# A two-layer encoder trunk: in layer 1 the weights of the strips and gate pairs are split one step sooner, the latent norms run piece by piece, and value tiles and the second key strip stand in front of the rope strip

## The chip, the cores and the metric

The kernel runs on one core of a Trainium2 chip. A core has a matrix engine (TensorE, "PE" in the profile), a vector engine ("DVE"), a scalar engine ("ACT"), a general engine ("POOL") and a queue that issues most DMAs ("SP"). Each engine works through its own list of instructions strictly in order and waits on semaphores for the others. The metric is the device time of one execution in microseconds; lower is better. The kernel before takes 1453.56 us (median of 3 runs, 1452.67 to 1453.84).

## What is computed

A sequence of 1024 tokens of width 1024 goes through two layers and a final RMSNorm. Both layers have an adaLN modulation, a SiLU gate z and a gated residual add. Layer 0 mixes tokens by differential attention, layer 1 by multi-head latent attention. Only layer 1 is touched by the change:

```python
proj = h @ w_in                      # q_a (384) | c_kv (256) | k_pe (64) | z (1024)
q  = (_rmsnorm(q_a, q_a_norm_g) @ w_q_b).reshape(b, s, 8, 128 + 64)
q_nope = q[..., :128]; q_pe = _rope(q[..., 128:], positions)
k_pe = _rope(k_pe[:, :, None, :], positions)[:, :, 0]
kv = (_rmsnorm(c_kv, kv_a_norm_g) @ w_kv_b).reshape(b, s, 8, 128 + 128)
k_nope, v = kv[..., :128], kv[..., 128:]
sc = (q_nope @ k_nope^T + q_pe @ k_pe^T) * scale      # per head
o  = softmax(sc) @ v
y  = (o.reshape(b, s, 1024) * silu(z)) @ w_out
x  = x + gate * y                    # then the final RMSNorm
```

## The kernel before

**Number format.** Every operand of a product is held as a pair of fp32r tiles, "hi" (the rounded value, suffix `h`) and "lo" (what is left, suffix `l`). One product is three matmuls (`mm3`: hi by hi, hi by lo, lo by hi; L180 to L182). A tile is 128 partitions by 512 values. Activations are kept transposed (features on partitions, tokens in two halves of 512).

**Weights.** A weight strip is 128 columns of the input projection. It comes in two pieces of 256 KB (`fetch_strip`, tile `wraw`, two buffers). `split_raw` makes the pair of a piece: ACT casts the hi tile (`wh`, L225), POOL subtracts for the lo tile (`wl`, L226). The pairs live in a ring of six tiles (tag `whl`). `gen_half` then runs one half of the tokens against one strip in eight steps of three matmuls; `side.tick()` after each step lets pending small work out of a queue (`side`).

**Layer 1, in order.** Layer 1 takes its strips in this order: k_pe (which goes through rope), the gates z of heads 0 and 1 (strips 6 and 7), and the two strips of c_kv (4 and 5). Beside these, `combos()` prepares sums of the activations (`t1` to `t4`, on DVE and ACT). Then come three gate pairs (`z_pair`), each two heads by seven products of 12 matmuls in the manner of Strassen; their weights (`zraw`, then the sums of them at L1372 to L1375) come from `z_weights`. Next are the three strips of q_a, with value tiles between them, then the key, rope and query strips of the heads (`kn`, `qr`, `qn`), and the attention loop, which uses later strips as filler between its steps (`stream1`).

**Latent norms.** `lora` normalises c_kv (2 tiles of features, `craw` to the pair `ck`) and q_a (3 tiles, `cqr` to `cq`), for each half of the tokens. The chain of one half is: sums of squares, `cps` (four tiny matmuls, L1302), `c_w` on DVE (L1304), `rq_y` on POOL (L167), a DMA `bc_d` to memory (L403), a DMA `bc_s` that broadcasts it back to all partitions (L405), one multiplication of each feature tile on DVE (L1311), and the split on ACT and DVE (L1319, L1320). The pieces of this chain stand in a list `norms`, and `run_norms()` issues what is in it at chosen places.

**Value tiles.** `v1_tile(tt, fh)` is six matmuls into `vps`; ACT and DVE make `v_hl` from it (L357, L358) and a DMA stores it. There are 8 token tiles for each of two halves `fh` of the value columns; I call those of fh 0 t0 to t7 and those of fh 1 f0 to f7. `load_wk` loads their weights (`wvr`, in the same two buffers as the strips) and splits them: `wvh` on DVE (L1436) and `wvl` on POOL (L1437).

**What sets the order.** The order in which the program is written decides most, then a scheduler places each engine's instructions from it. Accumulators (`acc`, `zacc`, `vps`) rotate through five PSUM banks here, so a product waits until the one five back has been read out by ACT and DVE.

## Time and profile before

| | |
|---|---|
| time, median of 3 runs | 1453.56 us (1452.67 to 1453.84) |
| profiled execution, its own time | 1448.94 us |
| span inside that execution | 1447.2 us |
| PE busy | 1392.7 us, 96% |
| PE weight loads | 1161.4 us, 80% |
| DVE busy | 913.5 us, 63% |
| ACT busy | 733.6 us, 51% |
| POOL busy | 609.6 us, 42% |

The profiled execution is 1.74 us longer than its span and 4.62 us (0.32%) shorter than the median. Times below are microseconds from the start of the span. A row of a timeline gives the start, the duration, the engine, the line, the operation, output and input tiles and, in square brackets, how long the engine stood idle before it and which instruction released it. Matmuls are pipelined: a row's duration is longer than the step from one start to the next, and where a length of matmuls is meant, the text goes by starts.

### The profile page before, as it was taken

The page shows a single profiled execution, that of the slowest core. Times are in us where ns is not written, and L with a number is a line of the kernel's source. Part 1 is how long each engine was busy: PE and PEld are TensorE (multiplying, and loading weights), DVE is VectorE, ACT ScalarE, POOL GpSimd, SP SyncE. Part 2 cuts the span into 40 slices and gives each one's busy share as a digit, 9 for nine tenths or more (in the row PEclk, how much of TensorE's full clock was granted, in tenths as well). Part 3 has the DMA queues.
Part 4 walks back from the last instruction along what each step waited for, and adds up shares of the span by engine and source line. Part 5 has one row for each costly group of instructions (what it writes and reads, how often), then busy time and mean ns, then how long its engine had stood idle before and what let it go on. Part 6 is the DMA issues. An engine that isn't in the chain of part 4 may idle for free.

```text
span 1447.2 us, 20558 instructions
## 1 busy us (share of the span) xinstructions
PE 1392.7 (96%) x7388; PEld 1161.4 (80%) x7388; DVE 913.5 (63%) x1360; ACT 733.6 (51%) x1299; POOL 609.6 (42%) x483
## 2 busy tenths in 40 slices
PE   5999999999999999998999998988999999999997
PEld 4777788888888887887787776867888888888886
DVE  6657877767777767677355965254666555555355
ACT  5622375656566655566344533334454554545442
POOL 4415164656465555553651246312141321412562
PEclk9999999999999999999999999999999999999999
DMA  9788823333332424237753322565343432336663
GB/s 330 231 258 231 254 72 96 81 98 91 100 92 83 110 74 116 57 91 263 235 164 131 88 73 88 163 175 138 119 127 114 122 101 76 104 96 215 216 206 138
DMA packets 129766, 203.20 MB, mean 140 GB/s; under 512 B 18432, under 2 KB 55424, under 8 KB 129664
## 3 DMA queue, kind: packets, MB, share of 16 engines
q1 hardware_dynamic: 129664, 201.89, 46.1%
q8 instruction: 58, 0.95, 0.3%
q14 instruction: 44, 0.36, 0.1%
HBM read 132.68 MB, written 45.56 MB: 123 GB/s over the span
## 4 chain that ended last, share of the span: by engine, by line
PE 78%; DMA 7%; DVE 6%; issue 3%; ACT 2%; POOL 2%; SPq 1%; ACTq 0%; POOLq 0%; DVEq 0%
PE s L1567 10%; PE acc L182 8%; PE acc L181 8%; PE acc L180 8%; PE tr L378 7%; PE s L769 7%; PE pv L180 4%; PE pv L181 4%; PE pv L182 4%; PE oacc L181 3%; PE oacc L180 3%; PE oacc L182 3%; DMA wvr<-in_w_v 1%; PE zacc L182 1%; DMA ada<-in_ada_ss 1%
## 5 line engine op out<-in xcount | busy, mean ns | idle before, releaser
L380 ACT CAST pth<-tr 128x512 fp32r<-128x512 f32 x256 | 150.1, 587 | 283.9 <-PE tr L378 279.4
L395 DVE TENSOR_REDUCE nm<-s 128x1 f32<-128x1024 f32 x192 | 233.8, 1218 | 74.0 <-PE s L769 64.1
L381 DVE TENSOR_TENSOR ptl<-tr,pth 128x512 fp32r<-128x512 f32 x256 | 175.9, 687 | 139.3 <-ACT pth L380 138.6
L226 POOL TENSOR_TENSOR wl<-wraw,wh 128x512 fp32r<-128x512 f32 (+2 forms) x82 | 104.0, 1270 | 216.3 <-ACT wh L225 197.2
L378 PE MATMUL tr<-ident,e 128*128 128x128 f32 x1024 | 155.1, 274 | 5.8 <-ACT e L397 3.8
L378 PEld LDWEIGHTS tr<-ident,e 128*128 128x128 f32 x1024 | 121.5, 141 | 46.4 <-DVE ptl L381 18.6
L397 ACT ACTIVATE e<-s,nm 128x1024 f32<-128x1024 f32 x128 | 143.5, 1121 | 28.6 <-DVE nm L395 28.2
L180 PE MATMUL acc<-h0h,wh 128*128 128x512 f32 x360 | 150.0, 417 | 3.6 <-DVE v_hl L358 2.6
L180 PE MATMUL pv<-pth,vt 128*128 128x256 f32 x512 | 147.2, 288 | 0.0
L181 PE MATMUL pv<-ptl,vt 128*128 128x256 f32 x512 | 145.8, 285 | 0.0
L182 PE MATMUL pv<-pth,vt 128*128 128x256 f32 x512 | 144.7, 283 | 0.0
L182 PE MATMUL acc<-h0h,wl 128*128 128x512 f32 x360 | 142.2, 395 | 0.2 <-POOL wl L226 0.2
L181 PE MATMUL acc<-h0l,wh 128*128 128x512 f32 x360 | 141.4, 393 | 0.0
L1009 POOL TENSOR_TENSOR wol<-wor,woh 128x512 fp32r<-128x512 f32 x64 | 85.2, 1350 | 84.4 <-ACT woh L1008 79.1
L180 PEld LDWEIGHTS pv<-pth,vt 128*128 128x128 f32 x512 | 97.6, 191 | 3.1 <-ACT pth L380 0.4
L181 PEld LDWEIGHTS pv<-ptl,vt 128*128 128x128 f32 x512 | 97.7, 191 | 2.6
L182 PEld LDWEIGHTS pv<-pth,vt 128*128 128x128 f32 x512 | 97.7, 191 | 0.1
L322 POOL TENSOR_TENSOR rp_r<-rp_raw,cosT 128x512 f32<-128x512 f32 x38 | 49.8, 1310 | 98.4 <-ACT rp_raw L317 51.9
L327 POOL TENSOR_TENSOR rp_sw<-rp_sw,sinT 128x512 f32<-128x512 f32 x42 | 56.0, 1333 | 78.0 <-DMA rp_sw<-rp_raw 73.3
L769 PE MATMUL s<-ks,qa 128*128 128x512 f32 x256 | 82.0, 402 | 3.0 <-DVE e L777 2.6
L777 DVE SCALAR_TENSOR_TENSOR e<-s,z,e 128x1024 f32<-128x1024 f32 x64 | 82.1, 1283 | 2.1
L769 PE MATMUL s<-ks,qb 128*128 128x512 f32 x256 | 80.9, 394 | 0.0
(600 smaller groups left out, 3344.2 us busy)
## 6 DMA issues: line engine op xcount, KB each, us to landing
ada<-in_ada_ss SPq DMA_DIRECT2D x32, 512.0 KB, 6.0
wraw<-in_w_s SPq DMA_DIRECT2D x64, 256.0 KB, 3.0
vS<-v_hl SPq DMA_DIRECT2D x32, 512.0 KB, 5.0
vt<-vS SPq DMA_DIRECT2D x32, 512.0 KB, 3.8
wor<-in_w_out SPq DMA_DIRECT2D x64, 256.0 KB, 4.1
rp_sw<-rp_raw SPq DMA_DIRECT2D x168, 64.0 KB, 2.0
bc_s<-bc_d SPq DMA_DIRECT2D x34, 256.0 KB, 4.2
oS<-bc_s SPq DMA_DIRECT2D x30, 256.0 KB, 2.9
```

The costliest lines, as they stand in the source:

```text
L180: PE.matmul(psum, ah, bh, start=first, stop=False)
L181: PE.matmul(psum, ah, bl, start=False, stop=False)
L182: PE.matmul(psum, al, bh, start=False, stop=last)
L226: sub = (V if pair_of else G).tensor_sub(l_[:, :n], raw[:, :n], f32v(h_[:, :n]))
L378: PE.transpose(tr[:, j, :], p[:, kt * P : (kt + 1) * P], ident)
L380: mk["S"] = S.copy(pth[kh][:, :, dst], tr).ins
L381: mk["V"] = V.tensor_sub(ptl[kh][:, :, dst], tr, f32v(pth[kh][:, :, dst])).ins
L395: mk["V"] = V.reduce_max(nm, s_ps, axis=AX.X, negate=True).ins
L397: mk["S"] = S.activation(e, s_ps, AF.Exp, bias=nm, scale=1.0, accum_out=zs).ins
L769: PE.matmul(s_ps[:, kc * HF : (kc + 1) * HF], src[:, c, ql], KS[h][kc][:, c, :], start=fst, stop=not fst)
L1009: in_turn(G.tensor_sub(lo, raw, f32v(hi)))
L1567: PE.matmul(s_ps[:, kc * HF : (kc + 1) * HF], lhs, rhs(kc), start=i == 0, stop=i == 4)
```

## The change

The computation, the instructions and their counts are the same; their order in layer 1 is not.

- `half_and_norm` becomes `run_half`, which takes hooks at given steps; `ahead()` fetches the next strip's two pieces and splits them at steps 0 and 5 of the half before it. The combos go out at every second tick, not every fourth, and `G_LATE` puts one more empty tick ahead of a group of h chunks.
- `lora`: for c_kv, scaling and split go out one feature tile at a time. For q_a the three scalings still go together.
- `z_weights` issues three of the four sums of a gate pair's weights at once, in front of its first split; `z_fetch(p + 1)` fetches all four pieces together. `load_wk(1)` moves from behind gate pair 1 to the end of pair 3, next to `load_wk(0)`.
- The second key strip goes ahead of the first rope strip and the first query strip. The q_a steps are dealt out 8 after each of the first four value tiles of fh 0 (4 after each of eight before), so the last four of them, which stood ahead of the norm of q_a, now stand beside and behind it.

```diff
@@ -45,7 +45,8 @@
 V_LATE = 6
 MODS = (2, 2, 2, 2, 3, 2, 0, 0)
 QA_V = 16
-V1_AT = ((2, 4), (3, 6), (0, 6), (1, 0))
+V_IN = 4
+V1_AT = ((2, 4), (3, 4), (0, 6), (0, 6))
 OT1_AT = 5
 NORM_AT = 4
 PRE0 = (0, 0, 0, 0, 0, 0, 1, 1, 1, 2, 1)
@@ -58,7 +59,7 @@
 Z_LAST = 4
 FILL7 = ((0, 1, 1, 1, 1, 0),) * 4
 G_WAIT = 3
-G_LATE = 2
+G_LATE = 3
 G1_AT = 7
 VB = (2, 5)
 WV1 = 6
@@ -1267,12 +1268,24 @@
             norms.remove(f)
             f()
 
-    def half_and_norm(w, half, consume):
+    def run_half(w, half, consume, at={}):
 
         for k, _ in enumerate(gen_half(w, h1, half, consume)):
             side.tick()
             if k == NORM_AT:
                 run_norms()
+            if k in at:
+                at[k]()
+
+    def ahead(raws):
+
+        hi, lo = [], []
+
+        def part():
+            for a, b in zip((hi, lo), split_raw(*raws.pop(0))):
+                a += b
+
+        return (hi, lo), {0: part, 5: part}
 
     def lora(n, dst, gvec, width, raw, part, lag):
 
@@ -1305,19 +1318,22 @@
             y = rsqrt(wv, 4)
             _, rb = bcast_rows(wp, y, "rp", 6)
 
-            def scale():
-                for i in range(n):
-                    t = craw[i][half]
-                    tc.keep_in_program_order(V.scalar_tensor_tensor(
-                        out=t3(t), in0=t3(t), scalar=gvec[:, i : i + 1], in1=rb, op0=ALU.mult, op1=ALU.mult))
-                norms.append(split)
-
-            def split():
-                for i in range(n):
-                    t = craw[i][half]
-                    dst[i][half] = hi, lo = part(), part()
-                    S.copy(hi, t)
-                    V.tensor_sub(lo, t, f32v(hi))
+            def scale(i=0):
+                t = craw[i][half]
+                tc.keep_in_program_order(V.scalar_tensor_tensor(
+                    out=t3(t), in0=t3(t), scalar=gvec[:, i : i + 1], in1=rb, op0=ALU.mult, op1=ALU.mult))
+                if i + 1 < n:
+                    if n == 2:
+                        norms.append(lambda: scale(i + 1))
+                    else:
+                        scale(i + 1)
+                norms.append(lambda: split(i))
+
+            def split(i):
+                t = craw[i][half]
+                dst[i][half] = hi, lo = part(), part()
+                S.copy(hi, t)
+                V.tensor_sub(lo, t, f32v(hi))
 
             norms.append(scale)
 
@@ -1338,40 +1354,36 @@
     cg = combos()
     side.add(None, g0)
     for i in range(16):
-        side.add(None, None, lambda: next(cg), None)
-    half_and_norm(w4[0], 1, lambda acc: side.q.insert(8, kp_half(1, acc)))
-    half_and_norm(w4[1], 1, z_put(0, 1))
-    w = strip1(7)
-    for half in range(2):
-        half_and_norm(w, half, z_put(1, half))
+        side.add(None, lambda: next(cg), None)
+    raws = fetch_strip([A["w_s1"][7, f] for f in range(2)], [4, 4])
+    run_half(w4[0], 1, lambda acc: side.q.insert(8, kp_half(1, acc)))
+    w, at = ahead(raws)
+    run_half(w4[1], 1, z_put(0, 1), at)
+    run_half(w, 0, z_put(1, 0))
+    raws = fetch_strip([A["w_s1"][4, f] for f in range(2)], [4, 4])
+    w_, at = ahead(raws)
+    run_half(w, 1, z_put(1, 1), at)
+    w = w_
     zraw = []
 
-    def z_fetch(p, parts):
-        for m, f in parts:
+    def z_fetch(p):
+        for m, f in ((0, 0), (0, 1), (1, 0), (1, 1)):
             raw = p4.tile([P, HF], F32, name="zraw", tag="zraw", bufs=6)
             SP.dma_start(raw, A["w_s1"][6 + 2 * p + m, f])
             zraw.append(raw)
 
-    for i in range(2):
-        w = strip1(4 + i)
-        for half in range(2):
-            half_and_norm(w, half, lambda acc: ckput(i, half, acc))
-            if i and not half:
-                z_fetch(1, ((0, 0), (0, 1), (1, 0), (1, 1)))
-    side.flush()
-
     def z_weights():
 
         for _ in range(1, NH // 2):
-            a11, a12 = zraw[:2]
-            yield split_raw(a11, 4)
-            yield split_raw(a12, 4)
-            a21, a22 = zraw[2:4]
+            a11, a12, a21, a22 = zraw[:4]
             del zraw[:4]
+            w_ = split_raw(a11, 4)
             s1 = p4.tile([P, HF], F32, name="zs1", tag="zraw", bufs=6)
             V.tensor_add(s1, a21, a22)
             V.tensor_sub(a21, a11, a21)
             V.tensor_sub(a11, s1, a11)
+            yield w_
+            yield split_raw(a12, 4)
             V.tensor_sub(a12, a12, a11)
             for t in (a11, a21, s1, a22, a12):
                 yield split_raw(t, 4)
@@ -1387,7 +1399,15 @@
 
     qraw = []
     zw = z_weights()
-    zq = [next(zw), next(zw)]
+    zq = []
+    run_half(w, 0, lambda acc: ckput(0, 0, acc))
+    w_, at = ahead(fetch_strip([A["w_s1"][5, f] for f in range(2)], [4, 4]))
+    run_half(w, 1, lambda acc: ckput(0, 1, acc), at)
+    side.flush()
+    z_fetch(1)
+    run_half(w_, 0, lambda acc: ckput(1, 0, acc))
+    run_half(w_, 1, lambda acc: ckput(1, 1, acc), {k: lambda: zq.append(next(zw)) for k in (0, 5)})
+
     def product(rhs):
 
         hi, lo = zq.pop(0)
@@ -1408,7 +1428,7 @@
         V.tensor_add(u, product(TC[2]), u)
         late(0)
         if more:
-            z_fetch(p + 1, ((0, 0), (0, 1)))
+            z_fetch(p + 1)
         acc = product(TC[3])
         u3 = rpt("zu3")
         V.tensor_add(u3, acc, u)
@@ -1419,8 +1439,6 @@
         V.tensor_add(u, acc, u)
         gate_out(2 * p + 1, 1, c_, c_)
         late(2)
-        if more:
-            z_fetch(p + 1, ((1, 0), (1, 1)))
         V.tensor_add(u3, product(TC[4]), u3)
         gate_out(2 * p + 1, 0, u3, u3)
         V.tensor_add(u, product(h1q(1, 1)), u)
@@ -1454,9 +1472,9 @@
             qraw.extend(fetch_strip([A["w_s1"][1, f] for f in range(2)], [4, 4]))
         if i == 2:
             load_wk(0)
+            load_wk(1)
 
     z_pair(1, late_z)
-    load_wk(1)
     z_pair(2, late_z)
     z_pair(3, late_q)
     st4.close()
@@ -1546,6 +1564,9 @@
         if h % 2 == 0:
             items.insert(len(items) - 1, (strip_l1("w_qr", h // 2, 3), CQ, qp_done(h)))
         steps1.append(16 if h % 2 == 0 else 10)
+    items[4:7] = [items[6], items[4], items[5]]
+    steps1[0] += 4
+    steps1[1] -= 4
     stream1 = Stream(gen_strips(items, wqa))
 
     def scores1(h, half, ti, zz):
@@ -1617,13 +1638,12 @@
     stream1.step(QA_V)
     for tt in range(NT):
         v1_tile(tt, 0, p4)
-        stream1.step(4)
-        if tt % 2:
-            run_norms()
+        run_norms()
+        if tt < V_IN:
+            stream1.step(32 // V_IN)
     st4.close()
     sth.close()
     ap = pool(st5, "attn1")
-    stream1.step(0)
     v1_left = list(range(NT))
     for n, steps in V1_AT:
         for tt in v1_left[:n]:
```

Three places show how the instructions now stand. Line numbers after the change are higher than before (L1311 becomes L1323, L1374 becomes L1384).

The first is DVE between gate pairs 1 and 2. `craw` is the scaling of c_kv's tiles, `zu` and `z` (L1385 before, L1397 after) belong to the gates, and the last row in each makes the weight tile that pair 2's third product needs. Before:

```order
L1311 SCALAR_TENSOR_TENSOR craw<-craw,vec,bc_s 128x512 x2
L1419 TENSOR_TENSOR zu<-zacc,zu 128x512
L1385 SCALAR_TENSOR_TENSOR z_8522<-zth,z_8522 128x512
L1320 TENSOR_TENSOR ck<-craw,ck 128x512
L1424 TENSOR_TENSOR zu_8488<-zacc,zu_8488 128x512
L1320 TENSOR_TENSOR ck<-craw,ck 128x512
L1311 SCALAR_TENSOR_TENSOR craw<-craw,vec,bc_s 128x512 x2
L1385 SCALAR_TENSOR_TENSOR zu_8488<-zth,zu_8488 128x512
L1426 TENSOR_TENSOR zu<-zacc,zu 128x512
L1436 CAST wvh<-wvr 128x512
L1374 TENSOR_TENSOR zraw<-zs_8600,zraw 128x512
```

After the change:

```order
L1323 SCALAR_TENSOR_TENSOR craw<-craw,vec,bc_s 128x512
L1439 TENSOR_TENSOR zu<-zacc,zu 128x512
L1397 SCALAR_TENSOR_TENSOR z_8525<-zth,z_8525 128x512
L1323 SCALAR_TENSOR_TENSOR craw<-craw,vec,bc_s 128x512
L1336 TENSOR_TENSOR ck<-craw,ck 128x512
L1323 SCALAR_TENSOR_TENSOR craw<-craw,vec,bc_s 128x512
L1384 TENSOR_TENSOR zraw<-zs_8542,zraw 128x512
```

The weight sum stood nine rows behind the first scalings, and one of the nine was a cast of value weights, which has left this place; now it stands six rows behind, and the scalings come one at a time.

The second is the norm of q_a. On DVE (`cqr` L1311 or L1323 is the scaling, first of token half 0, then of half 1), before:

```order
L1304 TENSOR_SCALAR c_w<-cps 128x4
L358 TENSOR_TENSOR v_hl<-vps,v_hl 128x512 x2
L1510 TENSOR_TENSOR kn_l<-acc,kn_h 128x512
L1311 SCALAR_TENSOR_TENSOR cqr<-cqr,vec,bc_s 128x512 x3
L1320 TENSOR_TENSOR cq<-cqr,cq 128x512
L1510 TENSOR_TENSOR kn_l<-acc,kn_h 128x512
L1320 TENSOR_TENSOR cq<-cqr,cq 128x512
L358 TENSOR_TENSOR v_hl<-vps,v_hl 128x512
L1320 TENSOR_TENSOR cq<-cqr,cq 128x512
L1311 SCALAR_TENSOR_TENSOR cqr<-cqr,vec,bc_s 128x512 x3
L1320 TENSOR_TENSOR cq<-cqr,cq 128x512
```

After:

```order
L1317 TENSOR_SCALAR c_w<-cps 128x4
L359 TENSOR_TENSOR v_hl<-vps,v_hl 128x512 x3
L1323 SCALAR_TENSOR_TENSOR cqr<-cqr,vec,bc_s 128x512 x3
L1528 TENSOR_TENSOR kn_l<-acc,kn_h 128x512
L1336 TENSOR_TENSOR cq<-cqr,cq 128x512
L1528 TENSOR_TENSOR kn_l<-acc,kn_h 128x512
L1336 TENSOR_TENSOR cq<-cqr,cq 128x512 x2
L1323 SCALAR_TENSOR_TENSOR cqr<-cqr,vec,bc_s 128x512 x3
L359 TENSOR_TENSOR v_hl<-vps,v_hl 128x512 x2
```

The first scalings now stand behind three value tiles of fh 0 (t5, t6, t7; `kn_l` follows them), and the scalings of half 1 stand in front of the read-out of f0 and f1. On PE in the same stretch, before, the last value tile is followed by the rope strip on `cq`:

```order
L180 MATMUL vps_9371<-wvh_8589,ck_8664 128x512
L181 MATMUL vps_9371<-wvl_8590,ck_8664 128x512
L182 MATMUL vps_9371<-wvh_8589,ck_8665 128x512
L180 MATMUL vps_9371<-wvh_8595,ck_8668 128x512
L181 MATMUL vps_9371<-wvl_8596,ck_8668 128x512
L182 MATMUL vps_9371<-wvh_8595,ck_8669 128x512
L180 MATMUL acc_9382<-cq_9294,wh_9324 128x512
L181 MATMUL acc_9382<-cq_9295,wh_9324 128x512
L182 MATMUL acc_9382<-cq_9294,wl_9325 128x512
```

After, the value tile f4 (`vps_9371`), the first half of the second key strip (`acc_9382`), and f3 (`vps_9360`), which takes over the bank of f0:

```order
L181 MATMUL vps_9371<-wvh_8887,ck_8683 128x512
L182 MATMUL vps_9371<-wvl_8888,ck_8683 128x512
L183 MATMUL vps_9371<-wvh_8887,ck_8684 128x512
L181 MATMUL acc_9382<-ck_8533,wh_9336 128x512
L182 MATMUL acc_9382<-ck_8534,wh_9336 128x512
L183 MATMUL acc_9382<-ck_8533,wl_9337 128x512
L181 MATMUL acc_9382<-ck_8647,wh_9336 128x512
L182 MATMUL acc_9382<-ck_8648,wh_9336 128x512
L183 MATMUL acc_9382<-ck_8647,wl_9337 128x512
L181 MATMUL vps_9360<-wvh_8881,ck_8533 128x512
L182 MATMUL vps_9360<-wvl_8882,ck_8533 128x512
L183 MATMUL vps_9360<-wvh_8881,ck_8534 128x512
```

So the matmuls on `cq` come later, and a value tile whose bank is freed behind the scalings of half 1 comes ahead of them.

The third is PE ahead of the first transpose of the attention loop (`tr`, of the exponentials `e`). Before, after the last score matmuls (`s1`):

```order
L1567 MATMUL s1_9500<-kps0_7010,qpb_9416 128x512
L1567 MATMUL s1_9500<-kps1_7011,qpb_9416 128x512
L1567 MATMUL s1_9547<-kps0_7010,qpb_9416 128x512
L1567 MATMUL s1_9547<-kps1_7011,qpb_9416 128x512
L182 MATMUL acc_9613<-ck_8668,wl_9469 128x512
L378 MATMUL tr_9566<-ident_79,e_9513 128x128 x4
```

After:

```order
L1588 MATMUL s1_9575<-kps1_7011,qpb_9444 128x512
L182 MATMUL acc_9601<-cq_9257,wh_9496 128x512
L183 MATMUL acc_9601<-cq_9256,wl_9497 128x512
L181 MATMUL acc_9679<-cq_9290,wh_9496 128x512
L182 MATMUL acc_9679<-cq_9291,wh_9496 128x512
L183 MATMUL acc_9679<-cq_9290,wl_9497 128x512
L181 MATMUL acc_9679<-cq_9286,wh_9496 128x512
L182 MATMUL acc_9679<-cq_9287,wh_9496 128x512
L183 MATMUL acc_9679<-cq_9286,wl_9497 128x512
L181 MATMUL acc_9679<-cq_9282,wh_9496 128x512
L182 MATMUL acc_9679<-cq_9283,wh_9496 128x512
L379 MATMUL tr_9594<-ident_79,e_9530 128x128 x4
```

One matmul of a key strip stood between the scores and the transpose; now ten of a query strip stand there (the second key strip has gone ahead).

## The prediction

> **What bounds the kernel now.** I read the page first: the shares of the engines and the chain that ended last.
>
> ```profile
> PE 1392.7 (96%) x7388; PEld 1161.4 (80%) x7388; DVE 913.5 (63%) x1360; ACT 733.6 (51%) x1299; POOL 609.6 (42%) x483
> PE 78%; DMA 7%; DVE 6%; issue 3%; ACT 2%; POOL 2%; SPq 1%; ACTq 0%; POOLq 0%; DVEq 0%
> ```
>
> PE bounds the kernel, and the change gives it the same matmuls. It can only win what PE loses, so the next view is PE's waits between 785 and 1000 us, the stretch where the order changes (columns: who waited for what, total, times, longest).
>
> ```profile
> PE tr L378 <- ACT e L397: 3.8, 1, 3.8
> PE zacc L182 <- POOL wl L226: 2.4, 1, 2.4
> PE zacc L180 <- ACT wh L225: 2.3, 1, 2.3
> PE acc L181 <- DVE cq L1320: 2.2, 3, 1.6
> PE acc L180 <- ACT cq L1319: 2.2, 1, 2.2
> PE acc L182 <- POOL wl L226: 1.5, 2, 0.9
> PE trh L484 <- DVE xfull L473: 0.8, 1, 0.8
> ```
>
> Idle time is not all of it. The timeline of PE, and two stretches of 2 us with the granted clock (the column after POOL's), show what follows the long waits.
>
> ```profile
> 862.61 0.39 PE L180 MATMUL zacc<-h_0h,wh 128*128 128x512 f32 x1
> 870.71 0.79 PE L180 MATMUL zacc<-t2h,wh 128*128 128x512 f32 x1 [2.33 <-ACT wh L225]
> 874.33 0.79 PE L182 MATMUL zacc<-t2h,wl 128*128 128x512 f32 x1 [2.40 <-POOL wl L226]
> 889.22 0.39 PE L180 MATMUL zacc<-h_0h,wh 128*128 128x512 f32 x1
> 908.54 0.39 PE L180 MATMUL acc<-h_0h,wh 128*128 128x512 f32 x1
> 963.82 0.39 PE L182 MATMUL vps<-wvh,ck 128*128 128x512 f32 x1
> 973.16 0.79 PE L180 MATMUL acc<-cq,wh 128*128 128x512 f32 x1 [2.22 <-ACT cq L1319]
> 981.41 0.40 PE L180 MATMUL vps<-wvh,ck 128*128 128x512 f32 x1
> 992.67 0.39 PE L182 MATMUL acc<-ck,wl 128*128 128x512 f32 x1
> 996.84 1.03 PE L378 MATMUL tr<-ident,e 128*128 128x128 f32 x4 [3.78 <-ACT e L397]
> 976.00:978.00 2.00, 2.00 (x7) 1.52 (x6) 2.00 (x4) 0.00 (x0) 0.00 (x0) 0.50 0.43 124
> 998.00:1000.00 2.00, 2.00 (x6) 1.52 (x5) 0.69 (x1) 0.53 (x1) 0.00 (x0) 0.50 1.01 284
> ```
>
> Each wait of 2.2 us or more is followed by matmuls at half clock (0.50); the longest single wait without it is 1.6. So I count losses by starts. **Place B**, gate pair 2, takes 889.22 - 862.61 = 26.61 us; pair 3, the same 84 matmuls, takes 908.54 - 889.22 = 19.32, or 0.23 each. Lost: 7.3. **Place C**, the rope and query strip, is 36 matmuls between the last value matmul (963.82) and the next one (981.41): 17.59 for 37 steps of 0.23, 8.5. Lost: 9.1. From 973.16 to 981.41 there are 19 matmuls (4.4 us) and 0.4 of idle time in 8.25, so half clock alone is 3.4 of it; at B what the two idle rows leave of 7.3 is 2.6. **Place D**, the first transpose: 996.84 - 992.67 - 0.23 = 3.9, and some 3.4 us of work at 0.50 behind it, 1.6. Lost: 5.5. Together 21.9 us are there to be won.
>
> **The change part by part.** The sum is made against the profiled execution, 1448.94 us, of which the span is 1447.2; the runs' median, 1453.56, is 4.62 higher, and I put the difference that I find on the median.
>
> *Place B.* PE waits for the lo and hi tile of a summed weight. On its way are DVE's rows:
>
> ```profile
> 859.67 2.19 DVE L1311 SCALAR_TENSOR_TENSOR craw<-craw,vec,bc_s 128x512 f32<-128x512 f32 x2 [1.70 <-DMA bc_s<-bc_d]
> 861.77 0.68 DVE L1419 TENSOR_TENSOR zu<-zacc,zu 128x512 f32<-128x512 f32 x1
> 862.37 1.51 DVE L1385 SCALAR_TENSOR_TENSOR z<-zth,z 128x512 f32<-128x512 f32 x1
> 869.26 0.67 DVE L1374 TENSOR_TENSOR zraw<-zs,zraw 128x512 f32<-128x512 f32 x1
> 870.04 1.14 ACT L225 CAST wh<-zraw 128x512 fp32r<-128x512 f32 x2
> 869.48 3.39 POOL L1437 TENSOR_TENSOR wvl<-wvr,wvh 128x512 fp32r<-128x512 f32 x1 [6.15 <-DVE wvh L1436]
> 872.84 3.13 POOL L226 TENSOR_TENSOR wl<-zraw,wh 128x512 fp32r<-128x512 f32 x2
> ```
>
> In the new order the sum stands behind one scaling, zu, z, a scaling, ck, a scaling. `zu` still starts at 861.77, since it waits for its product; then 0.6 + 1.5 + 1.1 + 0.6 + 1.1 by these rows (the split like zu): the sum starts at 866.7 instead of 869.26. PE's first matmul came 870.71 - 869.26 = 1.45 behind that start, so it can come at 868.1, and PE is free at 870.71 - 2.33 = 868.4: no wait. For the lo tile POOL was held by `wvl`, 3.39 us, and this one leaves the place. The cast starts 0.8 behind the sum (870.04 - 869.26) and takes 0.57, and from `wl` (872.84) to the matmul (874.33) it is 1.5, so the lo matmul comes at 869.6, wanted at 868.9: 0.7, too short for half clock; if z takes the 0.7 of its neighbours rather than 1.51, nothing. I take 0.3 left. At the worst the sum waits for a late `bc_s` of half 1 and costs as much as one of the old waits with its clock, 2.4 + 2.6; at the best 0.
>
> *Place C.* PE waits for `cq`, that is for the norm: `rq_y`, `bc_d`, `bc_s`, the scalings.
>
> ```profile
> 952.64 0.95 PE L1302 MATMUL cps<-ones,csum 128*128 128x1 f32 x8
> 955.63 0.95 PE L1302 MATMUL cps<-ones,csum 128*128 128x1 f32 x8
> 954.90 0.33 SPq L403 DMA_DIRECT2D bc_d<-rq_y  x1
> 957.87 0.33 SPq L405 DMA_DIRECT2D bc_s<-bc_d  x1
> 962.52 3.25 DVE L1311 SCALAR_TENSOR_TENSOR cqr<-cqr,vec,bc_s 128x512 f32<-128x512 f32 x3 [2.40 <-DMA bc_s<-bc_d]
> 958.98 7.08 DMA bc_d<-rq_y
> 966.08 4.18 DMA bc_s<-bc_d
> 970.28 4.30 DVE cqr L1311 x3
> ```
>
> Let E be the end of the `cps` of half 1 (955.63 + 0.95 = 956.6 before). The matmuls that stand ahead of those on `cq` become 24 + 12 + 6 + 6 + 6 + 6 + 6 = 66, 15.2 us, against 33 (7.6) before; that is the gain. But the read-outs now stand behind the scalings on DVE. Half 0: its `cps` ends 2.2 ahead of E (six matmuls and the `cps` between), its scalings start 8.9 later as before (962.52 - 953.6), at E + 6.7, take 3.25, and with 0.7 for `kn_l` f4's bank is free at E + 10.7. PE is there after 42 matmuls, E + 9.5 (it goes on 0.1 ahead of E): it waits 1.2. Half 1: `bc_d` is issued at E + 2.4 as before (958.98 - 956.6). It landed after 7.08; the one of half 0 after 957.87 - 954.90 = 2.97. Three transfers go out around it as before, one of 256 KB and two of 512, so I take 6.2. `bc_s` takes 4.18 to 4.65 (962.52 - 957.87), I take 4.3; the scalings 3.25 to 4.30, I take 3.6. Then `v_hl` of f0, 0.7: E + 17.2. PE wants f3 after 54 matmuls, E + 12.3, and is 4.9 late, 1.2 of it from f4. Its own wait there, 3.7, is over 2.2, so half clock follows: 2.6 and 3.4 before, I take 2.8. Place C then loses **7.7**: from 1.2 (fast landing, no half clock) to 6.8 + 3.4 = 10.2 (slow ones). Behind the wait on DVE stand the other read-outs and `cq`, and PE waits for them in turn; they follow 0.6 apart (as `zu` and z do above), faster than six matmuls (1.4), so nothing more is late.
>
> [...]
>
> *Place D.* Before the first `tr` come scores, their maximum `nm` on DVE, and `e` on ACT.
>
> ```profile
> 994.33 2.35 DVE L395 TENSOR_REDUCE nm<-s 128x1 f32<-128x1024 f32 x2
> ```
>
> From `nm` to `tr` it is 996.84 - 994.33 = 2.5, and the hand-over from the scores, which no row shows by itself, adds 0 to 0.5; I take 0.4: 2.9. Now 2 score and 10 query matmuls lie in between, 2.8, and no read-out of a key strip stands ahead of `nm`. I take **0.4** lost (0 to 3, if the rope is late).
>
> *The rest.* In strips 4 and 5 DVE feeds the combos, and on ACT the late piece's cast has moved behind two more combo casts: the waits of 1.5 for `wl` grow by 0.5 (0 to 1.1). The h chunk behind `trh` comes later in PE's list, 0.7 of its 0.8 goes. The four value-weight pieces now stand in one row at strip 1, and a buffer of the two is free for the next piece when its `wvl` is done:
>
> ```profile
> wraw<-in_w_s SPq DMA_DIRECT2D x64, 256.0 KB, 3.0
> 905.04 0.33 SPq L1434 DMA_DIRECT2D wvr<-in_w_v  x1
> 1002.00:1050.00 48.00, 48.00 (x292) 40.94 (x291) 30.91 (x46) 25.45 (x47) 8.12 (x6) 1.00 0.32 104
> ```
>
> From 905.04 two pieces pass a buffer in 2 x (3.0 load + 0.4 cast + 1.6 `wvl`), then strip 2's takes 3.0 + 0.6 + 1.6: its lo tile is there at 920.2. PE wants it behind strip 1 and a value tile, 908.54 + 54 x 0.23 + 0.2 = 921.2: nothing lost while a load takes less than 3.3; a load of 4.0 each would cost 2. In the attention loop fill is spent a little earlier, while PE has no idle time there now (last row: 48.00 of 48). I put 0.5 on these two together (-1 to 2).
>
> Sum: -21.9 + 0.3 + 7.7 + 0.4 + 0.5 - 0.7 + 0.5 = **-13.2**. The profiled execution comes to 1435.7, the median to 1453.6 - 13.2 = **1440.4 us**.
>
> **The rivals.**
>
> 1. *The tiles cover the norm.* `bc_d` of half 1 lands in 2.97 as that of half 0 did; place C loses 1.2. 1440.4 - 6.5 = **1433.9**. For it: that landing. Against it: two value stores of 512 KB are issued just ahead, as before.
> 2. *The weight sum is not sooner.* The DVE takes the scaling of half 1 ahead of the sum; if its `bc_s` is late, the waits and half clock of B stay, 7.0: **1447.4**. Against it: in the rows of place B DVE's only wait for a DMA is the 1.70 ahead of the first scaling, and five rows lie between that one and the scaling of half 1.
> 3. *The new wait takes place C and D.* Slow landings (10.2), f4's wait over 2.2 with half clock of its own (3.4), and a rope so late that D keeps its 5.5: 5.9 + 5.1 more, **1451.4**, no change to be told. Against it: it needs all scalings at 4.30.
> 4. *Slower: the softmax is uncovered.* Ten matmuls of fill now go ahead of the first transpose; in the second and third sixteen transposes PE has 0 and 4 of fill where it had 1 and 8. A missed `e` costs what D did, 5.5. From three missed ones on (16.5) the gain is gone: **1456.9**. Against it: DVE and ACT are busy 30.91 and 25.45 of 48 us there, so scores run ahead.
>
> **How the numbers follow.** The forecast (1437 to 1443.5 by its bounds) has 0.57, rival 1 0.14, rival 2 0.13, rival 3 0.10, rival 4 0.06. The range from 1434.5 to 1449.5 leaves out most of rivals 3 and 4 and half of rival 1, 0.2. The measurement tells some 0.2% from no change, 2.9 us: the forecast, rivals 1 and 2 and 0.02 of rival 3 lie on the faster side, 0.86; 0.08 is no change; 0.06 slower.
>
> **What would show it.** Right at B: no idle row at the third product of pair 2, that pair about 19.3 us long, clock 1.00. At C: PE's wait is by DVE's `v_hl` or `kn_l`, not by `cq`, near 3.7 us at f3, with a clock of 0.50 behind it; a landing of `bc_d` near 6 us. At D: the first `tr` waits less than 1 us. Wrong: a clock of 0.50 in pair 2, a wait for `e` above 2 us, or one behind 1000 us. I would be most wrong if f3 did not wait.

## The result, and the profile after

| | before | after |
|---|---|---|
| median, four runs each on one chip | 1453.12 us (1448.80 to 1453.84) | 1441.24 us (1440.18 to 1442.47) |
| profiled execution, its own time | 1448.94 us | 1442.18 us |
| span inside it | 1447.2 us | 1440.4 us |

The ratio is 0.9927, 95% interval [0.9911, 0.9943]: 0.7% faster, and 0.8 us from the forecast of 1440.4. Later the changed kernel ran once more on another chip, beside nine runs of the kernel before: 1441.56 against 1448.41 us, ratio 0.9954 [0.9941, 0.9966]. So the gain is 7 to 12 us. The forecast started from the median of the first three runs, 1453.56; the kernel before had medians of 1448.4 to 1450.6 on other chips.

The page of the changed kernel: PE's busy time hardly moved, as the same matmuls run. The waits of PE between 785 and 1000 us, and behind that those between 1000 and 1200 us (columns: who waited for what, total, times, longest; three rows of 0.6 us or less are left out):

```profile
PE 1390.9 (97%) x7388; PEld 1162.7 (81%) x7388; DVE 911.3 (63%) x1360; ACT 732.4 (51%) x1299; POOL 607.5 (42%) x483
```

```profile
PE vps L181 <- DVE v_hl L359: 2.6, 1, 2.6
PE vps L181 <- DVE kn_l L1528: 2.4, 1, 2.4
PE acc L183 <- POOL wl L227: 1.0, 1, 1.0
PE tr L379 <- DVE ptl L382: 1.9, 2, 1.4
```

The waits for `cq`, for `e` and for the first summed weight are gone; two for read-outs stand in place C, and the last row is a new one in the attention loop, where the kernel before had no wait at all in that window. The timeline of PE at the same places, and two stretches with the granted clock (the column after POOL's):

```profile
843.49 0.40 PE L181 MATMUL zacc<-h_0h,wh 128*128 128x512 f32 x1
864.72 0.39 PE L181 MATMUL zacc<-h_0h,wh 128*128 128x512 f32 x1
876.23 0.50 PE L181 MATMUL zacc<-t1h,wh 128*128 128x512 f32 x1 [0.30 <-ACT wh L226]
877.59 0.50 PE L183 MATMUL zacc<-t1h,wl 128*128 128x512 f32 x1 [0.62 <-POOL wl L227]
885.53 0.40 PE L181 MATMUL zacc<-h_0h,wh 128*128 128x512 f32 x1
904.85 0.40 PE L181 MATMUL acc<-h_0h,wh 128*128 128x512 f32 x1
947.12 0.95 PE L1315 MATMUL cps<-ones,csum 128*128 128x1 f32 x8
960.14 0.50 PE L181 MATMUL vps<-wvh,ck 128*128 128x512 f32 x1 [2.44 <-DVE kn_l L1528]
967.33 0.50 PE L181 MATMUL vps<-wvh,ck 128*128 128x512 f32 x1 [2.57 <-DVE v_hl L359]
981.55 0.72 PE L1588 MATMUL s<-kn_h,qn_h 128*128 128x512 f32 x2
992.88 0.66 PE L379 MATMUL tr<-ident,e 128*128 128x128 f32 x4
1046.81 0.66 PE L379 MATMUL tr<-ident,e 128*128 128x128 f32 x4 [1.37 <-DVE ptl L382]
```

```profile
962.00:964.00 2.00, 2.00 (x6) 1.52 (x6) 1.96 (x3) 1.58 (x4) 0.98 (x1) 0.50 0.88 351
968.00:970.00 2.00, 2.00 (x6) 1.54 (x5) 1.67 (x3) 0.17 (x1) 0.00 (x0) 0.50 0.73 198
```

From such starts I take four lengths for every kernel below. Strip 0 is the k_pe strip, with which layer 1 begins; strip 1 is the first strip of q_a, behind the gate pairs. **B** is the three gate pairs, from pair 1's first `zacc` to strip 1: 904.85 - 843.49 = 61.36 here, 67.15 before. **C** is what is lost between the start of the second `cps` and the first score: the length less 0.81 for the `cps` and 0.23 for each matmul recorded in it (here 981.55 - 947.12 - 0.81 - 109 x 0.23 = 8.6). **D** is lost between the first score and the first `tr`, again with 0.23 per matmul. **Tail** is strip 1 to the end of the span: 1440.4 - 904.85 = 535.55, before 1447.2 - 908.54 = 538.66. The work of PE in the tail is the same in all kernels, and the start-up ahead of layer 1, which differs by up to 4 us from one execution to the next, is left out.

| kernel | B | C lost | D lost | tail | time against before on the same chip |
|---|---|---|---|---|---|
| before | 67.15 | 9.1 | 4.0 | 538.66 | |
| after | 61.36 | 8.6 | 0.3 | 535.55 | 0.9927 |
| value weights back | 63.60 | 8.8 | 0.3 | 535.84 | 0.9958 [0.9943, 0.9973] |
| value weights alone | 66.06 | 7.2 | 4.0 | 537.82 | 0.9995 [0.9985, 1.0005] |
| key strip back | 61.26 | 6.3 | 3.2 | 535.56 | 0.9929 [0.9910, 0.9949] |
| read-outs first | 61.42 | 6.8 | 0.1 | 532.38 | 0.9916 [0.9901, 0.9931] |
| sum late | 61.56 | 9.8 | 0.3 | 536.44 | one run |
| norm whole | 63.90 | 9.4 | 2.6 | 540.00 | one run |
| read-outs first, splits in order | 61.28 | 4.9 | 0.2 | 530.91 | 0.9893 [0.9871, 0.9915] |
| the same, key strip first, five tiles | 61.31 | 2.1 | 0.1 | 528.07 | 0.9900 [0.9879, 0.9922] |
| key strip and tiles back | 61.37 | 9.4 | 0.2 | 533.43 | one run |
| key strip first, old order | 61.28 | 3.3 | 4.3 | 533.04 | one run |
| after, once more | 61.14 | 9.2 | 0.3 | 536.00 | 0.9954 [0.9941, 0.9966] |
| key strip first, four tiles | 61.56 | 2.0 | 1.0 | 529.70 | 0.9891 [0.9876, 0.9906] |

The nine profiles with the changed kernel's gate pairs agree in B to 0.4 us. Three profiles have the changed kernel's program in the tail (it itself twice, and the run with the sum late): they differ by 0.9 there (535.55 to 536.44) and by 1.2 in C (8.6 to 9.8). The kernel before and the one with the value weights alone, which have the same order from the norm of q_a on, differ by 1.9 in C. Only differences above these are read. Each row is one profile. In the profiles the change won 0.43 us ahead of pair 1 (62.42 to 61.99 from strip 0 to pair 1), 5.79 in B and 3.11 in the tail: 9.3 us.

### The profile page after: what moved, and what is told of

Same layout as the page of the kernel before. It is cut to its first block, busy times and chain, and to the rows that moved or that the text cites. A ratio compares the mean times of both kernels' runs of the same rounds, so it can differ in the third digit from the quotient of the medians.

```text
span 1440.4 us, 20566 instructions
## 1 busy us (share of the span) xinstructions
PE 1390.9 (97%) x7388; PEld 1162.7 (81%) x7388; DVE 911.3 (63%) x1360; ACT 732.4 (51%) x1299; POOL 607.5 (42%) x483
```

## The experiments

### Place B: which part of the change won it

**The second group of value weights back between the pairs**, all else as changed (row "value weights back"):

```diff
-            load_wk(1)
     z_pair(1, late_z)
+    load_wk(1)
```

> The changed kernel, with the value weights of the second half loaded and split behind gate pair 1 again (as before), nothing else. In its order DVE makes the weight sum at the changed kernel's early place; only the two casts and the two POOL subtractions (3.39 us for the one in the trace of before) come back between pairs 1 and 2. Theory: place B needs both the early sum and a free POOL; here the hi tile is in time and a lo tile is late by at most the subtraction less its slack, so 1 to 3 us over the changed kernel: 1442 to 1444 us. Rival, POOL's subtraction alone made place B: the 5.8 us that the changed kernel's trace wins there are lost, 1447 us.

Measured: 1443.38 us, pairs 63.60, as the theory has it: 2.2 us of B are this move's here, where the rest of the change is in. **The move alone**, in the kernel before:

```diff
+            load_wk(1)
     z_pair(1, late_z)
-    load_wk(1)
```

> The kernel before, with only the load and split of those value weights moved to the end of gate pair 3. The weight sum on DVE stays at its late place but for one cast of 0.4 us. Theory (both are needed): the hi tile still comes 1.9 us late (2.33 less 0.4), the lo tile follows it without the second wait of 2.40, and the wait is short of what brings half clock, so place B wins 3 to 5 of its 7.3 us: 1448 to 1450 us against 1453. Rival, POOL's subtraction alone: no wait at B, 1447 us. Second rival, the place of the sum alone: 1453 us.

Measured: 1448.99 against 1450.09 us, no difference that can be told; pairs 66.06, 1.1 won, less than the theory has it. PE still waits for the summed weight, 4.0 us in all against 4.7 before:

```profile
870.37 0.50 PE L180 MATMUL zacc<-t2h,wh 128*128 128x512 f32 x1 [2.25 <-ACT wh L225]
872.85 0.50 PE L182 MATMUL zacc<-t2h,wl 128*128 128x512 f32 x1 [1.76 <-POOL wl L226]
```

So the rest came from the sum's place in the list or from the norm by pieces. Each was undone alone, **the sums behind the first two splits again**:

```diff
-            w_ = split_raw(a11, 4)
+            yield split_raw(a11, 4)
+            yield split_raw(a12, 4)
             s1 = p4.tile([P, HF], F32, name="zs1", tag="zraw", bufs=6)
...
-            yield w_
-            yield split_raw(a12, 4)
```

> The changed kernel with one part undone: the sums of a gate pair's weights are issued behind the first two splits, as before. The latent norms stay piece by piece, and the second group of value weights stays away from the pairs. Read from the segment of the three gate pairs (z pair 1 to strip 1): 61.4 us in the changed kernel, 66.1 with the second group moved away alone. Theory, the sum's place in the list is what counts: about 66, with PE's waits of some 2 us for the hi tile of a summed weight (zacc for wh) back in pair 2. Rival, the norm piece by piece is what counts, since it leaves DVE free for the sum: 61.4 to 62, no wait over 0.7 there.

and **both tiles of a norm scaled together and split together again**:

```diff
-            def scale(i=0):
-                t = craw[i][half]
+            def scale():
+                for i in range(n):
+                    t = craw[i][half]
...
-                if i + 1 < n:
-                    if n == 2:
-                        norms.append(lambda: scale(i + 1))
-                    else:
-                        scale(i + 1)
-                norms.append(lambda: split(i))
+                norms.append(split)
...
-            def split(i):
-                t = craw[i][half]
+            def split():
+                for i in range(n):
+                    t = craw[i][half]
```

> The changed kernel with one other part undone: both feature tiles of c_kv are scaled together and split together, as before; the sums of the weights stay early. Theory, the sum's place counts: the three pairs stay at 61.4 to 62.5 us. Rival, the pieces count: 65 to 66, with a wait for the hi tile of over 2 us in pair 2. If both this run and the one with the late sum stay near 61.4, either part alone is enough; if both go to 66, the two are needed together.

Measured: 61.56 with the late sum, as its rival has it; 63.90 with the whole norm, between its theory and its rival. Four kernels without the value weights in the way:

| | norm whole | norm by pieces |
|---|---|---|
| sum late | 66.06 | 61.56 |
| sum early | 63.90 | 61.36 |

The changed kernel and two that differ from it in one part each give the clean comparison: undoing the pieces costs 2.5 us, undoing the early sum 0.2, less than the profiles differ among themselves. The fourth, 66.06, is the kernel before with the value weights moved; it also has the old fetches of the gate weights and the old strips ahead of the pairs, so its distance of 4.5 to the late sum and of 2.2 to the whole norm is not the pieces' or the sum's alone. With the pieces in, the place of the sum no longer matters; how much the early sum is worth without them is not shown.

What is left in B, 1.5 us in pair 2 (885.53 - 864.72 against 19.32), is a later piece, by these rows of DVE and ACT in the changed kernel:

```profile
873.88 1.13 DVE L1323 SCALAR_TENSOR_TENSOR craw<-craw,vec,bc_s 128x512 f32<-128x512 f32 x1
```

```profile
875.04 0.62 ACT L1335 CAST ck<-craw 128x512 fp32r<-128x512 f32 x1 [3.25 <-DVE craw L1323]
875.56 0.61 ACT L226 CAST wh<-zs 128x512 fp32r<-128x512 f32 x1
```

ACT idles 3.25 us for the last scaling of the norm, and the cast of the third summed weight, `zs`, stands behind that cast in its line. PE's 0.30 and 0.62 are for it. The rest, 0.6, has no row of its own.

### Places C and D: the key strip, the value tiles, and the splits of q_a

**The key strip put back** behind the rope and query strips:

```diff
-V1_AT = ((2, 4), (3, 4), (0, 6), (0, 6))
+V1_AT = ((2, 4), (3, 6), (0, 6), (1, 0))
...
-    items[4:7] = [items[6], items[4], items[5]]
-    steps1[0] += 4
-    steps1[1] -= 4
```

> The changed kernel, with the second key strip behind the first rope and query strip again (the order of items, its step counts and the table of value tiles as before); the q_a steps and norms as changed. Theory: the second key strip's 12 matmuls cover the norm ahead of the rope strip and the ten query matmuls cover the softmax ahead of the first transpose. Without it the wait for e comes back with its half clock (5.2 us), and the wait for cq grows by 0 to 2.8: 1446 to 1449 us. Rival, the first transpose was late only because the norm was: no wait for e above 1 us, 1441 to 1443 us.

Measured: ratio 0.9929, tail 535.56, the changed kernel's own. The new place of the key strip won 2.9 us at D and cost 2.3 at C, and without it PE has no wait for `ptl` in the attention loop. It nets nothing that can be told. At D, without it:

```profile
987.70 0.66 PE L379 MATMUL tr<-ident,e 128*128 128x128 f32 x4 [3.01 <-ACT e L398]
```

**The value tiles, the norm's pieces between them and the q_a steps back as well**, so that of the change only the gate pairs and the new split of q_a stay. The diff writes that split one tile at a time, but the three pieces of a half go into `norms` together and one `run_norms()` issues all three, as before. What it changes for q_a is their order: 2, 1, 0, where the kernel before has 0, 1, 2.

```diff
-        run_norms()
-        if tt < V_IN:
-            stream1.step(32 // V_IN)
+        stream1.step(4)
+        if tt % 2:
+            run_norms()
...
+    stream1.step(0)
```

> The changed kernel with the place of the value tiles, of the norm's pieces between them, of the q_a steps and of the second key strip as in the kernel before; the gate pairs stay as changed, and q_a is still split one tile at a time. Strip 1 to the end took 538.7 us before, 535.6 in the changed kernel and 535.6 with the key strip alone put back. Theory, the regrouped value tiles are what won the 3.1 us: 538 to 539.5, with PE's wait at the rope strip for cq, not for v_hl. Rival, the one-tile split of q_a won them: 535 to 536.5.

Measured: tail 533.43, below both theories and 2.1 us below the changed kernel. The regrouped value tiles did not win the tail's 3.1 us; with the key strip they cost 2.1 of the 5.2 that the tail had won without them (538.66 to 533.43). C loses what it lost before, 9.4 against 9.1, mostly by waits for `cq` (the longest 3.41), but the wait of 3.78 at D is gone. DVE's rows show it. In the kernel before, the last addition of the rope's half 0 (`rp_r`) stood behind a `qn_l` that waited 4.06 for `qn_h` of ACT, and behind two value read-outs:

```profile
982.24 0.69 DVE L1518 SCALAR_TENSOR_TENSOR qn_l<-acc,qn_h 128x512 fp32r<-128x512 f32 x1 [4.06 <-ACT qn_h L1517]
983.60 0.69 DVE L358 TENSOR_TENSOR v_hl<-vps,v_hl 128x512 fp32r<-128x512 f32 x1 [0.67 <-ACT v_hl L357]
985.00 0.69 DVE L358 TENSOR_TENSOR v_hl<-vps,v_hl 128x512 fp32r<-128x512 f32 x1 [0.71 <-ACT v_hl L357]
985.61 0.68 DVE L331 TENSOR_TENSOR rp_r<-rp_r,rp_sw 128x512 f32<-128x512 f32 x1
```

Here it stands ahead of that `qn_l` and goes as soon as POOL has made its operand:

```profile
975.85 0.69 DVE L332 TENSOR_TENSOR rp_r<-rp_r,rp_sw 128x512 f32<-128x512 f32 x1 [4.92 <-POOL rp_sw L328]
976.46 0.68 DVE L1536 SCALAR_TENSOR_TENSOR qn_l<-acc,qn_h 128x512 fp32r<-128x512 f32 x1
```

The whole-norm run above says the same from the other side: it also has the splits of q_a in the order 0, 1, 2 again, and in it D lost 2.6, with a wait for `e`, and the tail grew to 540.00:

```profile
PE tr L379 <- ACT e L398: 2.4, 1, 2.4
```

That the order of the splits is behind it can be read from the programs. From the norm of q_a on, this kernel is the kernel before with the three splits turned round, and the whole-norm kernel is the changed kernel with them turned round; all other differences of order follow from that. No run turned them round with everything ahead of the norm left alone, and why the scheduler then places `rp_r` sooner is not shown.

### Place C: read-outs against the norm

In the changed kernel PE waits for `kn_l` and `v_hl`, which stand behind the scalings of q_a on DVE. **The scalings four runs of the list later**, behind the read-outs:

```diff
-            norms.append(scale)
+            f = scale
+            for _ in range((4, 4)[half] if n == 3 else 0):
+                f = lambda f=f: norms.append(f)
+            norms.append(f)
```

> The changed kernel, with the scalings of q_a (both halves) issued four value tiles later in the program, so that on DVE the read-outs of the first key strip and of the value tiles f0 and f1 stand ahead of them; the same work. Theory: PE's waits at f4 (2.44) and f3 (2.57) and the half clock behind each came only from read-outs behind the scalings on DVE; cq itself is ready in time. Then place C loses 0 to 2 instead of 8.5: 1433 to 1436 us, no row of PE waiting for kn_l or v_hl there. Rival, the norm's own DMAs and scalings are the bound: PE waits for cq instead, with half clock, 1439 to 1442 us.

Measured: 1436.88 us, tail 532.38, 3.2 better, but C still loses 6.8 of its 8.6. The read-outs no longer hold PE; `cq` does in their place, as the rival has it, though the time is below the rival's:

```profile
963.02 0.73 PE L181 MATMUL acc<-cq,wh 128*128 128x512 f32 x2 [1.80 <-ACT cq L1335]
965.33 0.79 PE L182 MATMUL acc<-cq,wh 128*128 128x512 f32 x1 [1.57 <-DVE cq L1336]
966.00:968.00 2.00, 2.00 (x6) 1.57 (x5) 2.00 (x3) 0.00 (x0) 0.00 (x0) 0.50 1.15 346
```

The list makes the three splits in the order 2, 1, 0, while the rope strip's first matmul reads tile 0. **The splits in the order 0, 1, 2**, on top of that:

```diff
-                norms.append(lambda: split(i))
+                if n == 2:
+                    norms.append(lambda: split(i))
+                elif i == 0:
+                    norms.extend([lambda j=j: split(j) for j in range(n)])
```

> The changed kernel with the read-outs ahead of the scalings of q_a, as in the run before of that name, and the three splits of q_a in the order 0, 1, 2 (now 2, 1, 0, so that the tile which the rope strip's first matmul reads is made last). Theory, PE's waits of 1.80 and 1.57 us for cq and the clock of 0.50 behind them came from that order: strip 1 to the end takes 528.5 to 530.5 us against 532.4 without the new order, waits for cq below 1 us each, and the time is 0.984 to 0.988 of the kernel before. Rival, all three scalings come too late whatever the order (bc_s lands late): 532 to 533, the waits for cq keep their sum of 3.4.

Measured: 1434.50 us, tail 530.91, 1.5 better; two waits of 0.74 and 1.71 for `cq` are left, so the theory was half right: the tail is shorter by more than profiles of one program differ, but the waits did not fall below 1 each. The ratios to the kernel before (0.9916 and 0.9893, on two chips) have intervals that overlap. **The first key strip ahead of the value tiles**, five of them in a row behind it:

```diff
-V1_AT = ((2, 4), (3, 4), (0, 6), (0, 6))
+V1_AT = ((0, 4), (5, 4), (0, 6), (0, 6))
```

> As the run with the splits in order, and the first key strip stands ahead of value tiles f0 to f4 (it stood behind f0 and f1). By the durations of the traces the two read-outs of the key strip are then off DVE before the scalings land, and five value tiles in a row cover the norm: one wait for cq of some 1.3 us is left in place C, no half clock. Theory: strip 1 to the end 526 to 528.5 us, time 0.982 to 0.986 of the kernel before, faster than all the others. Rival, five value tiles in a row bind PE by their own read-outs and stores (a bank of five is free only when ACT and DVE have read it): waits of vps for v_hl over 2 us and half clock, 531 to 534.

Measured: tail 528.07, as the theory has it, C loses 2.1, one wait, of 1.91; the ratio, 0.9900, is not what it has. Of four runs only the profiled one took 1432.96 us; the others took 1435.52 to 1436.62, median 1436.03, and that this kernel beats the one ahead of it is not shown. **The same with the old order of the splits:**

> As the run with the key strip first, but the three splits of q_a in the order 2, 1, 0 again. Theory, the order counts as it did without the key strip in front (1.5 us of strip 1 to the end, 532.4 against 530.9): 529.5 to 531.5, three waits for cq with a sum of 3.5 to 5. Rival, five value tiles in a row cover either order: 528 to 528.6, one wait for cq below 2.

Measured: tail 533.04, later than either theory. The waits for `cq` are small (0.94, 0.49, 0.96), so five tiles do cover that; PE stops later, between the scores, for a read-out of a value tile, with half clock behind it, which is D's 4.3. The order 2, 1, 0, which went with the shorter tail in the old arrangement of strips and tiles, goes with the longer one here and in the runs with the read-outs first:

```profile
978.53 0.53 PE L181 MATMUL vps<-wvh,ck 128*128 128x512 f32 x1 [2.41 <-DVE v_hl L359]
980.00:982.00 2.00, 2.00 (x6) 1.59 (x5) 0.00 (x0) 0.00 (x0) 0.00 (x0) 0.50 0.58 131
```

**Four tiles between the key strips instead of five**, with the splits in order:

```diff
-V1_AT = ((2, 4), (3, 4), (0, 6), (0, 6))
+V1_AT = ((0, 4), (4, 4), (1, 6), (0, 6))
```

> As the run with the key strip first, with four value tiles between the first key strip and the second instead of five, and the fifth ahead of the rope strip's second half. By the durations of the traces PE waits once for cq, 1.3 to 1.9 us, and place D has no wait. Theory, a single wait below 2 us is not followed by half clock (1.91 was not in the run with five tiles): strip 1 to the end 527 to 529, time 0.984 to 0.988. [...]

Measured: 1432.64 us (1432.25 to 1433.00), ratio 0.9891 [0.9876, 0.9906]; on the same chip the changed kernel took 1441.56 and the kernel before 1448.41. This version beats both, by 8.9 and 15.8 us. The ratio and the tail, 529.70, lie just above the theory's ranges, but its reading of place C holds: one wait of 1.70 is left there, with full clock (1.00) behind it, and the four runs spread over 0.75 us; at D there is a wait of 0.57 that the theory did not have. DVE reads the key strip out ahead of the scalings and finds `bc_s` landed:

```profile
966.00 0.50 PE L182 MATMUL acc<-cq,wh 128*128 128x512 f32 x1 [1.70 <-DVE cq L1339]
966.00:968.00 2.00, 2.00 (x9) 1.65 (x10) 2.00 (x4) 0.05 (x1) 0.00 (x0) 1.00 0.68 183
950.66 0.69 DVE L1534 TENSOR_TENSOR kn_l<-acc,kn_h 128x512 fp32r<-128x512 f32 x1 [0.90 <-ACT kn_h L1533]
953.75 3.25 DVE L1323 SCALAR_TENSOR_TENSOR cqr<-cqr,vec,bc_s 128x512 f32<-128x512 f32 x3
```

### The clock behind a wait

**The changed kernel once more**, for a second profile of its place C:

> The changed kernel once more, on the chip and beside the kernel of the next run, with a second profile of its place C. Theory, a wait of over 2.2 us is followed by half clock each time: both waits (for kn_l and for v_hl, 2.3 to 2.9 each) have 0.50 behind them again, place C loses 8 to 9.5, time 0.991 to 0.995 of the kernel before. [...]

Measured: the same wait of 2.44 for `kn_l`, and this time full clock behind it (1.00 in the last row), up to the wait for `v_hl`:

```profile
959.18 0.50 PE L181 MATMUL vps<-wvh,ck 128*128 128x512 f32 x1 [2.44 <-DVE kn_l L1528]
966.35 0.79 PE L181 MATMUL vps<-wvh,ck 128*128 128x512 f32 x1 [4.07 <-DVE v_hl L359]
960.00:962.00 2.00, 2.00 (x10) 1.41 (x8) 1.95 (x3) 2.00 (x5) 1.27 (x1) 1.00 0.99 383
```

In the first profile the 2.44 had 0.50 behind it (962 to 964 us). So the theory does not hold: a wait of the same length was followed by half clock in one profile and not in the other, and what decides it is not shown. The loss, 9.2, is no smaller for it and lies in the theory's range: PE came to the second wait sooner and stood there 4.07 instead of 2.57, as the read-out's end is set by DVE.

## Why the prediction was right, and where it was not

**The time** was right, the sum behind it too large: -13.2 against -9.3 in the profiles. The forecast was put on a median of 1453.6, which on other chips was 1448.4 to 1450.6; against the profiled execution it gave 1435.7, and that took 1442.18. That the two errors cancelled to 0.8 us is luck.

**Place B**, -7.0 predicted, -5.8 measured. The move of `wvl` brought 2.2 of the 5.8, and the waits at the third product are gone. The step that failed is "I take 0.3 left": it followed the first summed weight only, and the third one is now late, 1.5 us in all, behind the last piece of the norm on ACT. The prediction also did not say which part brings the sum forward on DVE: undone alone, the sum's own place in the list was worth 0.2 and the pieces of the norm 2.5.

**Place C**, 7.7 lost predicted, 8.6 measured, 9.2 the second time. What holds PE was named rightly: `kn_l`, then `v_hl` at f3. The times of the chain were off, by these rows of SP and DVE in the changed kernel (the second `cps` starts at 947.12):

```profile
947.09 0.33 SPq L404 DMA_DIRECT2D bc_d<-rq_y  x1
949.89 1.97 SPq L406 DMA_DIRECT2D bc_s<-bc_d  x1
951.96 0.39 SPq L404 DMA_DIRECT2D bc_d<-rq_y  x1
957.04 0.33 SPq L406 DMA_DIRECT2D bc_s<-bc_d  x1
```

```profile
956.28 3.20 DVE L1323 SCALAR_TENSOR_TENSOR cqr<-cqr,vec,bc_s 128x512 f32<-128x512 f32 x3 [4.03 <-DMA bc_s<-bc_d]
963.45 3.22 DVE L1323 SCALAR_TENSOR_TENSOR cqr<-cqr,vec,bc_s 128x512 f32<-128x512 f32 x3
966.58 1.29 DVE L359 TENSOR_TENSOR v_hl<-vps,v_hl 128x512 fp32r<-128x512 f32 x2
```

With E = 947.1 + 0.95 = 948.1, half 0's scalings were put at E + 6.7 = 954.8 and came at 956.28: `bc_s` took 6.4 us from its issue (956.28 - 949.89), not 4.65. That is f4's wait, 2.44 for 1.2. For half 1 the late landing of `bc_d` that the working was built on, and rival 1 with it, decided nothing: its scalings have no wait for a DMA in their row; on DVE they stand behind half 0's, two read-outs and three splits.

**Half clock at C** was taken as 2.8 behind a single wait; idle time is 5.0 (2.44 + 2.57) and the clock what is left of 8.6, 3.6, behind two. Which wait gets half clock differs from one execution to the next (behind the same 2.44 the clock was 0.50 in one profile and 1.00 in the other), so a single figure for it was not to be had. The rule read from the kernel before, that each wait of 2.2 us or more is followed by half clock, falls with that.

**Place D**, 0.4 lost predicted, 0.3 measured, and no wait. The reason was wrong in part. The key strip's new place does keep PE busy there when the value tiles are regrouped (without it, a wait of 3.0), but the wait is gone just as well with strip and tiles in their old place and the splits of q_a in the order 2, 1, 0. The prediction has no term for that order; with the order 0, 1, 2 and the norm of c_kv whole, the tail is 4.5 us longer (540.00 against 535.55).

**The rest**, +0.5 predicted with a bound of 2 for loop and value weights. From the tail: -3.1 is -0.5 at C (9.1 to 8.6, within what profiles of one program differ there), -3.7 at D, and +1.1. The 1.6 of half clock behind D's old wait are in that rest and are gone, so the loop lost 2.7. Its rows show 1.9, two waits for `ptl` (1046.81 above is the longer), and they are absent where the key strip is put back: rival 4's place and cause, fill spent early, though PE waits there for `ptl` and not for `e`, and 1.9 us where it had 16.5. The other 0.8 has no row of its own. Ahead of pair 1 the change won 0.43, against 0.2 predicted.

Rival 2 (the sum not sooner) is refuted at the place: the wait for the first summed weight is gone. Rival 3 (new waits take C and D) got C nearly right and D wrong.

## What to carry to other kernels

When a wait is taken from one engine's line by moving work ahead of it, list what now stands behind that work on the engine that serves it, each instruction with its own consumer: at C the read-outs behind the scalings cost as much as the waits they replaced, and putting them in front, with the splits in the order in which the matmuls read them and the first key strip ahead of four value tiles, won 8.9 us more, all three together. Undo each part of a change alone, and read its diff for what it really reorders: here strip and tiles, which stood for all of the gain expected at C and D, cost 2.1 us in the tail, and a side effect that no one had counted (the three splits of q_a in reverse order) went with a tail 5.2 shorter without them, and with a longer one once the read-outs stood first. So the worth of an order holds only beside what stands around it. Put a predicted difference on the profiled execution it was read from; the median of three runs lay 3 to 5 us above those on other chips.

## What the runs showed of the hardware

- The clock behind a wait did not go by its length alone. A wait of 2.44 had 0.50 behind it in one profile and 1.00 in another of the same kernel; 1.91 (five tiles) and 1.70 (four tiles) had 1.00, but 1.71 in the run with the splits in order had 0.50. What else decides it is not shown. The rows of the 1.71:

```profile
963.55 0.50 PE L182 MATMUL acc<-cq,wh 128*128 128x512 f32 x1 [0.74 <-DVE cq L1339]
969.54 0.65 PE L182 MATMUL acc<-cq,wh 128*128 128x512 f32 x1 [1.71 <-DVE cq L1339]
970.00:972.00 2.00, 2.00 (x6) 1.63 (x5) 2.00 (x5) 0.09 (x1) 0.00 (x0) 0.50 0.68 181
```

- Three executions of the run with five value tiles in a row took 2.6 to 3.7 us longer than its profiled one (1435.52 to 1436.62 against 1432.96). Their traces were not kept, so the cause stays open.
- The broadcast `bc_s` of half 0 in the changed kernel landed 6.4 us after its issue began, against 4.65 in the kernel before. Its issue alone took 1.97 us on SP instead of 0.33, but the one of half 1, issued in 0.33, took 5.8 as well.
